# A list scheduler's landing times for GpSimd's transfers, and weight sums spread over fewer weights, in a hybrid transformer block

## The chip, the cores and the metric

The kernel runs on one core of a Trainium2 chip, in one launch. The metric is the device time of one execution in microseconds (us); several executions are timed and the median is compared. One further execution was taken with the hardware profiler. The engines are named as the profile names them: PE (matrix products; PEld is its weight load), DVE (vector), ACT (scalar and activations), POOL (GpSimd) and SP (which only issues transfers here).

## The reference

One layer on 256 tokens of width 2048, everything in float32: two SwiGLU blocks (5632 wide) around a gated recurrence, a second recurrence and a cross attention, each with a norm ahead of it and a residual sum behind it.

```python
x = x + 0.5 * swiglu(rms_norm(x, ffn1_norm[l]), ffn1_w_up[l], ffn1_w_down[l])
h = rms_norm(x, mix_norm[l])
proj = h @ w_in[l]
...
merged = g[:, :, 0, :] * (y_a @ w_branch_a[l]) + g[:, :, 1, :] * (y_b @ w_branch_b[l])
x = x + merged @ w_out[l]
x = x + cross_attention(rms_norm(x, xattn_norm[l]), rms_norm(mem, mem_norm[l]), xattn_wq[l], xattn_wkv[l], xattn_wo[l])
x = x + 0.5 * swiglu(rms_norm(x, ffn2_norm[l]), ffn2_w_up[l], ffn2_w_down[l])
return rms_norm(x, final_norm)
```

## The kernel before

**Tiles.** Every weight comes in pieces of 128 x 2048 float32 (1 MB), loaded by SP into a tile `raw`. ACT copies a piece to a rounded type (`h`), DVE subtracts that from the piece (`l`, what the rounding lost), and PE multiplies both parts with the two parts of the activations, so that three cheap products stand for one float32 product (`split`, L531). The pieces are used in one fixed order (`plan`): the first feed forward block (`ffn1`), 176 pieces of the middle (the input projection, gates, branches, output, and the attention's four weights), and the second block (`ffn2`). The function `weights` (L584) takes the next piece and prepares the one after.

**Fewer products by sums of weights.** In both feed forward blocks most pieces of the up projection take part in a scheme that needs seven products where eight were needed, but with four differences of blocks of the weight (tile `td`). In `ffn2`, 36 pieces (list `MADE`, L47) have these differences made ahead, in the middle of the kernel: POOL loads a piece from `wu2` into a tile `made`, DVE does four subtractions of 128 x 512 in it, and POOL stores it to a place in device memory, `kept` (`make_sums`, L611). Later SP loads it from there into `td`. `make_ahead` (L603) says at which weight each of the 36 is recorded: evenly over `between[1]` = 170 weights from the third of the middle on, the subtractions and the store two weights behind the load. In `ffn1`, 24 pieces have `l` made by another way: ACT writes the negative of the rounded piece and POOL issues a transfer that adds the piece to it (`begin_added`, L626).

**Tiles in rings.** All 1 MB tiles (`raw`, `h`, `l`, `td`, `tl`, `own`, `made`, `ev`) come out of one ring of 9 buffers, with 4 more inside the two feed forward blocks. A new tile takes a buffer whose last user is done, in the plan described next. On the chip, the first instruction that writes the tile waits on semaphores until that user is really done.

**The order.** Nothing is issued as it is written. Each call is recorded as an `Op` with a cost (`price`, L254): time on its engine (`busy`) and, for a transfer, the time for which it holds the memory path (`moved`, 2.9 us a MB, 5.2 with an addition). `arrange` (L290) then works out the order of all operations: it goes through planned time, and gives each free engine the ready operation that is due first, counting back from PE's use of it. For a transfer, planned time says that its data are there, or its source is free, at `dma + 1.9`, where `dma` is the planned end of its share of the memory path (L382); the same 1.9 us stands in `spent`, from which due times come (L296). The result is the order of instructions on each engine, and which buffer each tile gets. Planned times themselves are not in the program: engines run their instructions in that order, and wait for each other by semaphores alone. `emit` (L434) issues all of it from one line, L464, so that the profile shows every instruction with that line; tiles tell them apart.

Of the kernel before, what the change touches and what calls it, by code (L numbers as in the profile page):

```python
# [46 lines left out]
MADE = [(g, p) for g in range(1, NG) for p in range(8) if p not in ((4, 6) if g < 3 else (1, 2, 3, 5, 6))]  # L47
# [131 lines left out]
LAG = {"PE": 0.24, "DVE": 0.15, "ACT": 0.16, "POOL": 0.16, "SP": 0.1}  # L179
# [4 lines left out]
class Flow:  # L184
# [69 lines left out]
    def price(self, op, method, args, kw, outs):  # L254
        q = op.queue.name
        n = outs[0].cells.size if outs else 0
        if method == "dma_start":
            n = n or args[1].cells.size
            op.moved = n * 512 / 2 ** 20 * (5.2 if "accum_op" in kw else 2.9)
            op.busy = 0.9 if q == "POOL" else 0.06  # L260
        elif method == "transpose":
            op.busy += 0.099
        elif q == "PE":
            op.busy += n / 2400 + 0.0137 if not op.turn else 0.021 if n <= 32 else 0.07 + n * 1.05e-3
        elif q == "DVE":
            n = max(n, kw["in_"].cells.size) if method == "tensor_reduce" else n
            per = {"reciprocal": 6.2, "tensor_tensor_scan": 2.2}.get(method, 1.042)
            op.busy = n * per / 1000 + 0.07
        elif q == "ACT":
            op.busy = n * 0.838e-3 + 0.095 + (0.1 if "accum_out" in kw else 0)  # L270
            op.table = args[2] if args[2] in TABLES else None
        else:
            op.busy = 1.0
# [16 lines left out]
    def arrange(self):  # L290
# [2 lines left out]
        ops = self.ops  # L293
        for op in ops:
            op.after = [a for a in getattr(op, "extra", ())]
            op.spent = op.busy + LAG[op.queue.name] + (op.moved + 1.9 if op.moved else 0)  # L296
        for op in ops:
            op.waits = len(op.deps)
            for d in op.deps:
# [20 lines left out]
        dma = reached = 0.0  # L320
# [6 lines left out]
        def enter(op):  # L327
            if op.nominal > reached + AHEAD:
                heappush(later[op.queue.name], (op.nominal, op.i, op))
            else:  # L330
                insort(cand[op.queue.name], op, key=lambda o: (o.due, o.i))
# [8 lines left out]
        while events:  # L340
            t, e = heappop(events)
            if free[e] > t + 1e-9:
                continue
            while later[e] and later[e][0][0] <= reached + AHEAD:
                enter(heappop(later[e])[2])
            best, soon = None, 1e18
            for op in cand[e]:
                if best is not None and (not last or best.turn or op.due - STICK > best.due):
                    break
                if best is not None and not op.turn:  # L350
                    continue
                r = op.ready
                if op.moved:
                    r = max(r, dma - BACKLOG)
                if r <= t + 1e-9:
                    for ring in {x.ring for x in op.takes}:
                        fit = ring.fit(op, self)
                        r = max(r, fit[-1][0] if fit else 1e18)
                if r <= t + 1e-9:
                    best = op  # L360
                else:
                    soon = min(soon, r)
            if best is None:
                if soon < 1e17:
                    heappush(events, (soon, e))
                continue
            op = best
            cand[e].remove(op)
            op.start = t
            sequence.append(op)  # L370
            busy = op.busy
            if op.table is not None and op.table != table:
                table = op.table
                busy += 1.3
            if e == "PE":
                busy += 0.1 * (op.turn != last)
                last = op.turn
            free[e] = t + busy
            op.end = t + busy + LAG[e]
            if op.moved:  # L380
                dma = max(dma, t + busy) + op.moved
                op.end = dma + 1.9  # L382
            woken = {e}
            if e == "PE" and op.nominal > reached:
                reached = op.nominal
                woken.update(names)
            for ring in {x.ring for x in op.takes}:
                fit = ring.fit(op, self)
                for x in op.takes:
                    if x.ring is ring:  # L390
                        f = fit.pop(0)
                        ring.take(op, f)
                        x.place = f[1]
                        scope = ring.places[f[1]][0].scope
                        if scope is not None:
                            self.opened = max(self.opened, scope)
                            live[scope] += 1
                        if f[2] is not None:
                            for u in f[2].users:
                                if u is not op:  # L400
                                    u.extra.append(op)
                woken.update(names)
            if op.scope is not None:
                live[op.scope] -= 1
            for x in op.tiles:
                x.left -= 1
                x.ends = max(x.ends, op.end)
                if not x.left:
                    x.ring.free.append((x.ends, x.place, x))
                    if x.ring.places[x.place][0].scope is not None:  # L410
                        live[x.ring.places[x.place][0].scope] -= 1
                    woken.update(names)
            for s in op.after:
                kind = s.deps[op]
                if kind is None:
                    r = t
                elif s.queue is op.queue and not op.moved:
                    r = t + busy + (0.1 if kind and e in ("DVE", "ACT") else 0)
                else:
                    r = op.end  # L420
                s.ready = max(s.ready, r)
                s.waits -= 1
                if not s.waits:
                    enter(s)
                    woken.add(s.queue.name)
            for n in woken:
                heappush(events, (max(t, free[n]), n))
            done += 1
# [40 lines left out]
def block_kernel(tc: tile.TileContext, xT, xin, memT, vec, gfin, bgate, lruw, wu1, wd1, win, wv,  # L469
# [91 lines left out]
    between = len(plan)  # L561
# [16 lines left out]
    between = between + 2, len(plan) - between - 6  # L578
# [5 lines left out]
    def weights(*key):  # L584
        while plan and len(ahead) < 2:
            i = next(planned)
            k, src, kind = plan.pop(0)
            flow.room = room["scope"] if k[0] in orders else None
            if i < len(head):
                head[i]()  # L590
            if plan and plan[0][2] == "added":
                begun.append(begin_added(plan[0][1]))
            ahead.append((k, prepare(src, kind, 4 if i < 4 else 1)))
            if i in rest:
                rest[i]()
            make_ahead(i - between[0])
        k, w = ahead.pop(0)
        assert k == key, (k, key)
        return w
# [1 line left out]
    sums_kept, makers = {}, []  # L601

    def make_ahead(i):  # L603
        n, pieces = len(MADE), between[1]
        if 0 <= i < pieces:
            for j in range(i * n // pieces, (i + 1) * n // pieces):
                makers.append((i + 2, make_sums(*MADE[j])))
        while makers and (makers[0][0] == i or i == pieces):
            makers.pop(0)[1]()

    def make_sums(g, p):  # L611
        raw = big("made", F32)
        r = [raw[:, i * 512:(i + 1) * 512] for i in range(4)]
        gps.dma_start(raw, wu2[g, p])

        def sums():
            for o, a, b in ((1, 0, 1), (0, 0, 2), (2, 2, 1), (3, 3, 2)):
                dve.tensor_tensor(out=r[o], in0=r[a], in1=r[b], op=ALU.subtract)
            kept = sums_kept[g, p] = dram.tile([P, 2048], F32, name=f"kept{g}_{p}", tag=f"kept{g}_{p}")
            gps.dma_start(kept, raw)  # L620

        return sums
# [1033 lines left out]
```

## Time and profile before

| | |
|---|---|
| time, median of 3 executions | 2453.64 us (2452.77 to 2455.08) |
| profiled execution, its own time | 2456.57 us |
| profiled execution, span from first to last instruction | 2454.8 us |
| granted clock of PE, mean | 0.997 of full |
| memory read and written | 538.13 MB and 39.85 MB |

A row of a group view of the profile has the operation with the tile that it writes and those that it reads (`out<-in`), its size and count; behind the bar the busy time in us and the mean of one in ns; then for how long its engine stood idle just before such instructions, and what ended that. A row of the timeline has start and duration in us; in brackets stands the idle time of the engine before it, and whom it waited for. A row of waits has the sum of such idle times, their number and the longest. A row of the table by stretches has the stretch, its length, busy time and instructions of PE, PEld, DVE, ACT and POOL, then PE's granted clock, the busy share of the transfer engines, and GB/s. `acc` is a bank of PE's accumulators; SPq marks SP's queue of transfers.

### The profile page before, as it was taken

Reading aid. Unit: us, or ns where it says so; the run is one execution under the profiler, and the core shown is the slowest. Engines: PE = TensorE matmul, PEld = TensorE weight load, DVE = VectorE, ACT = ScalarE, POOL = GpSimd, SP = SyncE. Lnnn points to the kernel's source line nnn. Section 1 sums busy time; section 2 is a strip of 40 time slices with the busy share of each in tenths; the row PEclk is TensorE's granted clock in tenths of the full one; section 3 lists DMA queues with packets and bytes.
Section 4 is the critical chain, followed back from the end, with each engine's and each line's share of the span. In section 5 each row is a group of like instructions: output and inputs, shape, how many; then the busy total and the mean of one; then the engine's idle time right before and its main releaser. Section 6 shows DMA issues by size and latency. Waiting matters only on the chain. (4 is left out here: it accounts for less than half of the span.)

```text
span 2454.8 us, 30751 instructions
## 1 busy us (share of the span) xinstructions
PE 2423.6 (99%) x12166; PEld 2018.0 (82%) x12166; DVE 2010.7 (82%) x2171; ACT 1405.8 (57%) x1408; POOL 61.7 (3%) x102
## 2 busy tenths in 40 slices
PE   9999999999999999999999999999999999999998
PEld 8888888888888887888788788888878788888887
DVE  8999999999855767687676777667769999999995
ACT  8566666666654443576434644545646566666663
POOL 0000000000000000000000000000000000000000
PEclk9999999999999999999999999999999999999999
DMA  8567888778745566767777676666787666666672
GB/s 308 188 228 257 257 260 254 257 251 264 243 152 196 203 243 218 275 242 272 260 269 268 241 292 243 259 227 232 290 321 286 242 244 244 244 244 244 244 287 111
DMA packets 89712, 605.14 MB, mean 247 GB/s; under 512 B 9952, under 2 KB 10208, under 8 KB 21472
## 3 DMA queue, kind: packets, MB, share of 16 engines
q1 hardware_dynamic: 75024, 501.38, 55.5%
q0 software_dynamic: 13824, 100.67, 13.3%
q8 instruction: 95, 1.56, 0.2%
q10 hardware_dynamic: 720, 1.13, 0.1%
q14 instruction: 49, 0.40, 0.0%
HBM read 538.13 MB, written 39.85 MB: 235 GB/s over the span
## 5 line engine op out<-in xcount | busy, mean ns | idle before, releaser
L464 DVE TENSOR_TENSOR l<-raw,h 128x2048 fp32r<-128x2048 f32 (+2 forms) x428 | 875.7, 2051 | 226.3 <-ACT h L464 115.8
L464 ACT ACTIVATE h<-raw 128x2048 fp32r<-128x2048 f32 (+2 forms) x428 | 736.6, 1725 | 536.0 <-PE acc L464 145.1
L464 PE MATMUL acc<-h,xh 128*128 128x512 f32 x1248 | 469.9, 391 | 2.8 <-ACT h L464 2.4
L464 PE MATMUL acc<-h,xl 128*128 128x512 f32 x1248 | 449.9, 389 | 0.0
L464 PE MATMUL acc<-h,hidop 128*128 128x512 f32 x1408 | 442.2, 390 | 0.0
L464 PE MATMUL acc<-h,ops 128*128 128x512 f32 x1664 | 412.5, 392 | 1.2 <-DVE gate L464 1.2
L464 ACT ACTIVATE h<-td 128x1024 fp32r<-128x1024 f32 (+1 forms) x244 | 286.8, 1182 | 208.3 <-DVE td L464 182.8
L464 PE MATMUL acc<-ops,h 128*128 128x512 f32 x1152 | 392.7, 398 | 0.4 <-DVE ops L464 0.4
L464 PEld LDWEIGHTS acc<-h,ops 128*128 128x128 f32 x1664 | 311.1, 188 | 65.5 <-DVE gate L464 1.5
L464 DVE TENSOR_TENSOR tl<-td,h 128x1024 fp32r<-128x1024 f32 (+1 forms) x244 | 333.0, 1373 | 22.1 <-ACT h L464 14.4
L464 PEld LDWEIGHTS acc<-h,hidop 128*128 128x128 f32 x1408 | 262.9, 188 | 53.9 <-ACT ev L464 0.2
L464 PE MATMUL acc<-ops,l 128*128 128x256 f32 x1152 | 273.6, 282 | 8.1 <-DVE l L464 8.1
L464 PEld LDWEIGHTS acc<-h,xh 128*128 128x128 f32 x1248 | 233.5, 188 | 56.1 <-ACT h L464 7.4
L464 PEld LDWEIGHTS acc<-h,xl 128*128 128x128 f32 x1248 | 234.3, 188 | 48.6
L464 PE MATMUL acc<-l,hidop 128*128 128x512 f32 x704 | 265.8, 389 | 0.0
L464 PEld LDWEIGHTS acc<-ops,l 128*128 128x128 f32 x1152 | 213.4, 190 | 29.0 <-DVE l L464 9.0
L464 PEld LDWEIGHTS acc<-ops,h 128*128 128x128 f32 x1152 | 203.2, 189 | 32.1 <-DVE ops L464 0.7
L464 PE MATMUL acc<-l,ops 128*128 128x512 f32 x832 | 221.0, 389 | 0.0
L464 PE MATMUL acc<-l,xh 128*128 128x512 f32 x688 | 198.8, 390 | 0.0
L464 PEld LDWEIGHTS acc<-l,ops 128*128 128x128 f32 x832 | 155.6, 188 | 32.2
L464 PE MATMUL acc<-tl,xh 128*128 128x512 f32 x560 | 174.3, 391 | 0.3 <-DVE tl L464 0.2
L464 PEld LDWEIGHTS acc<-l,hidop 128*128 128x128 f32 x704 | 132.2, 188 | 27.4
(172 smaller groups left out, 1893.2 us busy)
## 6 DMA issues: line engine op xcount, KB each, us to landing
raw<-wu SPq DMA_DIRECT2D x128, 1024.0 KB, 6.8
raw<-wd SPq DMA_DIRECT2D x72, 1024.0 KB, 6.3
raw<-win SPq DMA_DIRECT2D x40, 1024.0 KB, 4.8
made<-wu POOLq DMA_DIRECT2D x36, 1024.0 KB, 5.2
kept<-made POOLq DMA_DIRECT2D x36, 1024.0 KB, 6.2
td<-kept SPq DMA_DIRECT2D x36, 1024.0 KB, 6.6
raw<-wg SPq DMA_DIRECT2D x32, 1024.0 KB, 5.4
raw<-wu SPq DMA_DIRECT2D x36, 768.0 KB, 4.3
```

The lines of the kernel that those rows point to most:

```text
L464: getattr(op.queue.real, method)(*map(real, args), **{k: real(v) for k, v in kw.items()})
```

## The change

Two constants of planned time and one count change; no operation is added or removed.

- Planned landing is now a number for each transfer, `lands`: 1.9 us as before where SP or ACT issues it, and for POOL's transfers 3.2 us where it adds (the 24 of `ffn1`), 4.6 us for a load into `made`, and 5.8 us for a store from `made` to `kept`. (The line tells the load by its tiles: it touches no tile but the one that it writes.) It stands in both places where 1.9 stood.
- `make_ahead` spreads the 36 loads of `made` over 154 weights where it had 170.

```diff
@@ -258,6 +258,7 @@
             n = n or args[1].cells.size
             op.moved = n * 512 / 2 ** 20 * (5.2 if "accum_op" in kw else 2.9)
             op.busy = 0.9 if q == "POOL" else 0.06
+            op.lands = 1.9 if q != "POOL" else 3.2 if "accum_op" in kw else 4.6 if op.tiles - {args[0].tile} == set() else 5.8
         elif method == "transpose":
@@ -293,7 +294,7 @@
-            op.spent = op.busy + LAG[op.queue.name] + (op.moved + 1.9 if op.moved else 0)
+            op.spent = op.busy + LAG[op.queue.name] + (op.moved + op.lands if op.moved else 0)
@@ -379,7 +380,7 @@
                 dma = max(dma, t + busy) + op.moved
-                op.end = dma + 1.9
+                op.end = dma + op.lands
@@ -601,7 +602,7 @@
     def make_ahead(i):
-        n, pieces = len(MADE), between[1]
+        n, pieces = len(MADE), between[1] - 16
         if 0 <= i < pieces:
             for j in range(i * n // pieces, (i + 1) * n // pieces):
                 makers.append((i + 2, make_sums(*MADE[j])))
```

Since the whole order is worked out from these numbers, nearly every row of it moves somewhat. Two places are shown, both on DVE, both with the numbers of the tiles.

The first is in the middle of the kernel, in the last part of the input projection. `made` are the subtractions for the fourth piece of `MADE`; `l` is the lower part of a weight that PE takes next; `ya`, `ostd` and `plain` belong to the recurrences. In the order before:

```order
L464 TENSOR_TENSOR made_7274<-made_7274 128x512
L464 TENSOR_TENSOR ya_7283<-acc_7220,ostd_7332 128x256
L464 RECIPROCAL ostd_7332<-ostd_7332 128x256
L464 SCALAR_TENSOR_TENSOR ya_7283<-ya_7283,vt_74,silu_5987 128x256
L464 TENSOR_TENSOR ya_7283<-acc_7221,ostd_7332 128x256
L464 TENSOR_TENSOR plain_7337<-plain_7337,rstd_5469 128x256
L464 SCALAR_TENSOR_TENSOR ya_7283<-ya_7283,vt_74,silu_5987 128x256
L464 TENSOR_TENSOR plain_7337<-acc_7285,lo_7399 128x256
L464 TENSOR_TENSOR plain_7337<-plain_7337,rstd_5469 128x256
L464 TENSOR_TENSOR l_7414<-raw_7217,h_7270 128x2048
```

In the order now, of the same piece:

```order
L465 TENSOR_TENSOR made_7230<-made_7230 128x512
L465 TENSOR_TENSOR l_7333<-raw_7243,h_7307 128x2048
L465 TENSOR_TENSOR plain_7350<-acc_7210,lo_7331 128x256
L465 RECIPROCAL ostd_7338<-ostd_7338 128x256
L465 TENSOR_TENSOR plain_7350<-plain_7350,rstd_5469 128x256
L465 TENSOR_TENSOR ya_7255<-acc_7219,ostd_7338 128x256
L465 RECIPROCAL ostd_7338<-ostd_7338 128x256
L465 TENSOR_TENSOR l_7384<-raw_7284,h_7343 128x2048
...
L465 SCALAR_TENSOR_TENSOR ya_7255<-ya_7255,vt_74,silu_5987 128x256
L465 TENSOR_TENSOR l_7424<-raw_7353,h_7406 128x2048
```

`l_7414` before and `l_7424` now lie in the buffer from which the `made` of this place was stored, at one and the same address; eight small operations stood between the last subtraction and the new tile, and now there are twelve (four of them left out above), two of them splits of whole weights into other buffers.

The second place is the last of the 36 pieces. In the order before, its four subtractions (`made_14290`) stand among the splits of `ffn2`, where `tl` is the lower part of a `td`:

```order
L464 TENSOR_TENSOR l_14284<-raw_14232,h_14266 128x1536
L464 TENSOR_TENSOR tl_14314<-td_14252,h_14301 128x2048
L464 TENSOR_TENSOR l_14333<-raw_14274,h_14320 128x2048
L464 TENSOR_TENSOR made_14290<-made_14290 128x512 x4
L464 TENSOR_TENSOR l_14365<-raw_14307,h_14352 128x1536
L464 TENSOR_TENSOR tl_14386<-td_14323,h_14373 128x2048
```

Now they (`made_13692`) stand in the attention's output product, where `xs` and `xl` are the first operands of `ffn2` in the making:

```order
L465 TENSOR_TENSOR xs_13744<-xg_13731,xs_13744 128x128
L465 TENSOR_TENSOR xl_13762<-xg_13731,xh_13755 128x512
L465 TENSOR_TENSOR made_13692<-made_13692 128x512 x3
L465 TENSOR_TENSOR xl_13753<-xs_13744,xh_13742 128x512
L465 TENSOR_TENSOR l_13786<-raw_13710,h_13772 128x2048
L465 TENSOR_TENSOR made_13692<-made_13692 128x512
```

`l_13786` is the first weight of `ffn2`; PE's first product of that block stands behind these rows in the program. No load of `made` and no subtraction is left inside `ffn2`.

## The prediction

> **What bounds the kernel now.** I read the share of the engines first, then what PE waits for, then the table by stretches.
>
> ```profile
> span 2454.8 us, 30751 instructions
> PE 2423.6 (99%) x12166; PEld 2018.0 (82%) x12166; DVE 2010.7 (82%) x2171; ACT 1405.8 (57%) x1408; POOL 61.7 (3%) x102
> PE acc L464 <- DVE l L464: 8.1, 2, 5.6
> PE acc L464 <- DVE merge L464: 3.4, 3, 1.6
> PE acc L464 <- ACT h L464: 2.4, 3, 1.3
> PE acc L464 <- DVE p L464: 2.0, 2, 1.4
> PE acc L464 <- DVE hidop L464: 1.5, 3, 0.7
> PE acc L464 <- DVE x L464: 1.2, 3, 0.6
> PE acc L464 <- DVE gate L464: 1.2, 1, 1.2
> PE warm L464 <- DVE ones L464: 1.1, 1, 1.1
> 829.00:1837.00 1008.00, 989.72 (x5452) 831.15 (x5451) 713.05 (x858) 510.26 (x596) 39.60 (x73) 0.99 0.70 259
> 2000.00:2050.00 50.00, 50.00 (x226) 41.22 (x225) 49.90 (x47) 31.35 (x26) 0.00 (x0) 1.00 0.65 234
> ```
>
> PE is the bound: it is busy for 99% of the span, and the change gives it the same products. So the change can only move PE's idle time. The eight rows of its waits add up to 8.1 + 3.4 + 2.4 + 2.0 + 1.5 + 1.2 + 1.2 + 1.1 = 20.9 us. The stretch from 829 to 1837 us, in which all 36 pieces are made ahead, holds 1008 - 989.7 = 18.3 us of it. There DVE is busy for 71% and the transfer engines for 70%: the waits are a matter of order and not of load. In `ffn2` (2000 to 2050 us) PE and DVE are both full and PE does not wait.
>
> **The change part by part: landings.** What the constants are about can be compared with the trace.
>
> ```profile
> made<-wu POOLq DMA_DIRECT2D x36, 1024.0 KB, 5.2
> kept<-made POOLq DMA_DIRECT2D x36, 1024.0 KB, 6.2
> l<-own POOLq DMA_DIRECT2D x24, 1024.0 KB, 8.2
> DVE made L464 <- DMA made<-wu: 32.6, 15, 4.3
> DVE l L464 <- DMA kept<-made: 18.8, 8, 5.6
> SPq L464 <- DMA kept<-made: 89.6, 17, 9.6
> ```
>
> The code before books a load of `made` and a store of `kept` alike, 0.9 to issue + 2.9 + 1.9 = 5.7 us, and an adding transfer 0.9 + 5.2 + 1.9 = 8.0. Now it books 0.9 + 2.9 + 4.6 = 8.4, 0.9 + 2.9 + 5.8 = 9.6 and 9.3. The medians of the last column (issue to landing) are 5.2, 6.2 and 8.2, so the old booking is short for about half of them, and the trace shows who pays: DVE stood 15 times before subtractions whose piece had not landed, and 8 times before a split whose buffer was still being stored. Mostly nobody needed DVE just then. Three times PE did.
>
> **A, 939 us.**
>
> ```profile
> 915.53 0.53 POOL L464 DMA_DIRECT2D made<-wu  x1 [19.14 <-PE acc L464]
> 923.03 1.42 DVE L464 TENSOR_TENSOR made<-made 128x512 f32<-128x512 f32 x2 [2.94 <-DMA made<-wu]
> 928.00 0.54 POOL L464 DMA_DIRECT2D kept<-made  x1 [11.93 <-DVE ya L464]
> 937.35 4.49 DVE L464 TENSOR_TENSOR l<-raw,h 128x2048 fp32r<-128x2048 f32 x2 [5.61 <-DMA kept<-made]
> 939.69 0.58 PE L464 MATMUL acc<-ops,l 128*128 128x256 f32 x1 [5.55 <-DVE l L464]
> 939.00:945.00 6.00, 5.31 (x18) 4.63 (x19) 6.00 (x4) 1.91 (x1) 0.00 (x0) 0.52 0.45 175
> ```
>
> The load took 923.0 - 915.5 = 7.5 us until DVE could begin, and the store 937.35 - 928.0 = 9.35; DVE lost 2.94 and 5.61 us to them, and PE, which needed that split, 5.55. Then PE's clock is down: 0.52 over six microseconds, of which PE ran 5.31, so 0.48 x 5.3 = 2.5 us more. The new bookings (8.4 and 9.6) cover both. The order now bears that out: behind the last subtraction stand, ahead of the split that takes this buffer, two splits into other buffers more than before. One such split costs 4.49 / 2 = 2.2 us, so DVE has 4.5 us more work to do while the store lands. That leaves 5.61 - 4.5 = 1.1 us, and DVE comes there with the 2.94 us of the load's wait saved. I take all: -5.55 - 2.5 = **-8.1**. If the wait only moved to the next split, it would be 0.
>
> On the clock the Trainium skill ("TensorE: Matmul & The Clock Gate", Part 1) says that PE falls to half clock after an idle window of about 3.4 us. For the 5.55 us here the trace agrees. For the two waits under D, of 1.6 us each, it would give no loss, and the trace shows one; by the page the sum would be 0.9 us smaller, and the measurement decides.
>
> **B, 1044 us, and C, 1403 us.**
>
> ```profile
> 1034.12 0.53 POOL L464 DMA_DIRECT2D made<-wu  x1 [10.72 <-PE acc L464]
> 1041.98 1.42 DVE L464 TENSOR_TENSOR made<-made 128x512 f32<-128x512 f32 x2 [2.70 <-DMA made<-wu]
> 1044.12 1.20 PE L464 MATMUL acc<-h,ops 128*128 128x512 f32 x4 [1.21 <-DVE gate L464]
> 1394.74 0.54 POOL L464 DMA_DIRECT2D kept<-made  x1 [11.80 <-DVE sum L464]
> 1401.33 2.29 DVE L464 TENSOR_TENSOR l<-raw,h 128x2048 fp32r<-128x2048 f32 x1 [1.55 <-DMA kept<-made]
> 1403.67 1.57 PE L464 MATMUL acc<-ops,l 128*128 128x256 f32 x11 [2.56 <-DVE l L464]
> ```
>
> B: subtractions 7.9 us behind the issue of their load (booked 5.7, now 8.4), and the gate product queued behind them on DVE. C: a split 6.6 us behind its store (booked 5.7, now 9.6). Both are covered: **-1.2** and **-2.6**.
>
> **D, 1211 us.**
>
> ```profile
> 1201.47 1.92 ACT L464 ACTIVATE h<-raw 128x2048 fp32r<-128x2048 f32 x1 [7.14 <-DMA raw<-wab]
> 1211.37 0.33 PE L464 MATMUL acc<-vt,merge 128*128 128x128 f32 x1 [1.56 <-DVE merge L464]
> 1213.30 0.98 PE L464 MATMUL acc<-vt,merge 128*128 128x128 f32 x7 [1.59 <-DVE merge L464]
> 1210.00:1218.00 8.00, 5.03 (x19) 3.99 (x20) 7.79 (x10) 1.09 (x2) 0.53 (x1) 0.79 0.79 297
> ```
>
> Weights came late (ACT stood 7.14 us for one), the splits ran into the merge, and PE lost 1.56 + 1.59 + 0.21 x 8 = 4.8 us. SP's queue waits for stores of `kept` 17 times in all, which a later booking avoids by giving loads other buffers; but PE waits for `merge` by its very chain. I take half, **-2.4**, with 0 and -4.8 as ends.
>
> **E, the spread: 1826 us.** One piece per 154/36 = 4.3 weights where it was 4.7, and the last ones no longer in `ffn2`.
>
> ```profile
> DMA packets 1940, 13.14 MB, mean 375 GB/s; under 512 B 209, under 2 KB 209, under 8 KB 721
> kept<-made POOLq DMA_DIRECT2D x1, 1024.0 KB, 11.8
> made<-wu POOLq DMA_DIRECT2D x1, 1024.0 KB, 9.3
> raw<-wu SPq DMA_DIRECT2D x2, 1024.0 KB, 11.6
> 1826.36 0.50 PE L464 MATMUL acc<-h,xh 128*128 128x512 f32 x1 [0.90 <-ACT h L464]
> 1830.97 0.50 PE L464 MATMUL acc<-h,xh 128*128 128x512 f32 x1 [1.33 <-ACT h L464]
> ```
>
> From 1800 to 1835 us (the first four rows are of that stretch) the transfers run at 375 GB/s, and single ones take 9 to 12 us. POOL's are 3 MB of the 13; without them, 3.1 MB / 375 GB/s = 8 us of transfers, the weights land earlier than PE waited: **-2.2**. The price is a denser middle. The 144 subtractions go by at 0.69 us at most (1.42 for two above), 99 us in 1008; at 170/154 the rate, that is 1.0 point of DVE's share more, beside 29% free, and the transfers rise from 259 to about 266 GB/s. I cost it at nothing; if that cover failed, what is pushed is a split of 2.2 us.
>
> **F, the rest of the order.** `ffn1`'s adding transfers are booked 1.3 us longer. They were booked right on the median, and PE waits there for little (at most the 1.5 us of `hidop`): 0. But a new order draws its small waits anew. Those not named above are 20.9 - 1.1 (start) - 5.55 - 1.2 - 2.6 - 3.15 - 2.2 = 5.1 us. At best none comes, at worst they take back all; I take some half of 5.1 as added, **+3**.
>
> Sum: -8.1 - 1.2 - 2.6 - 2.4 - 2.2 + 3 = -13.5 us on a span of 2454.8. The profiled execution itself took 2456.57, 2.9 above the median shown, so I take the difference and not the level: 2453.6 - 13.5 = **2440 us**. The floor is with no wait but the first: 20.9 - 1.1 + 2.5 + 1.7 = 24 us less, 2430.
>
> **The rivals.** *The old booking was long enough*, and what DVE waited for is contention, which goes wherever the transfers go. For it: E shows 9 to 12 us for transfers of one size. Against it: right behind A the transfer engines are busy for 0.45 only, and the stores' median is above 5.7. Then A to D reappear elsewhere, only E remains: about 2451 us.
>
> The Trainium skill ("DMA: Bandwidth & Descriptors", Anatomy of one DMA, SWDGE path) would have it so: by its fit, 2.0 us + bytes / 436e3, a transfer of 1 MB takes an estimated 4.4 us, which either booking covers. The medians here, 5.2 and 6.2, disagree.
>
> *Loads come late* (slower). A buffer of `made` is now booked 2.7 + 3.9 = 6.6 us longer in each of 36 rounds, out of nine buffers; SP then issues the weights' loads later, and where one lands late ACT, DVE and PE wait in turn, as at D, for 4.8 us each. It needs four such stalls to eat up A to E, and a fifth and sixth to be seen: some 2460 us. For it: the 7.14 us of ACT above, SP's 89.6 us. Against it: most of the booked time was spent waiting anyway, and the middle has 30% of its transfer time free.
>
> *All waits go* (faster): the order is right nearly everywhere, F is zero or below, D goes fully: 2432 us.
>
> **How the numbers follow.** A difference below about 0.2%, 4.9 us, can't be told from none here. The sum's case (2434 to 2447) gets 0.60, all waits gone 0.13, old booking enough 0.16, loads late 0.11. So faster 0.73; within 0.2%, 0.16; slower 0.11. The range for 8 of 10 goes from the floor's neighbour, 2431, to 2452, which takes in the second case.
>
> **What would show it.** In the waits, DVE's for `made` and for `kept` (32.6 and 18.8 us) fall below a third, and SP's 89.6 falls. PE's waits from 829 to 1837 us fall from 18 to some 5 us, and no stretch there has a clock of 0.5. From 1800 to 1835 us POOL issues nothing, and the raw weights land in under 9 us. Wrong would be: DVE's waits gone but PE's as long, for `h` behind late loads (the slower rival), or waits for `made` as before (the first). Wrong of another kind: a loss in `ffn2`, where DVE has nothing free and a start behind time would never be made up.

## The result, and the profile after

The changed kernel takes 2432.78 us (median of 4, 2430.61 to 2433.69) where the kernel before took 2453.72 beside it: 20.9 us or 0.85% less, ratio 0.9913 with a 95% interval of 0.9896 to 0.993. That lies inside the range, below the predicted 2440 and next to the case called "all waits go" (2432). The profiled execution took 2433.69 us, its span 2431.9, which is 22.9 less than the span before.

The page of the changed kernel, its first lines, then all of PE's waits (sum, number, longest):

```profile
span 2431.9 us, 30728 instructions
PE 2417.1 (99%) x12166; PEld 2014.7 (83%) x12166; DVE 2013.4 (83%) x2171; ACT 1410.1 (58%) x1408; POOL 61.5 (3%) x102
PE acc L465 <- DVE tl L465: 1.5, 2, 0.9
PE warm L465 <- DVE ones L465: 1.1, 1, 1.1
PE acc L465 <- DVE merge L465: 0.8, 1, 0.8
PE acc L465 <- ACT h L465: 0.5, 2, 0.3
PE acc L465 <- DVE hidop L465: 0.5, 1, 0.5
PE acc L465 <- ACT ev L465: 0.3, 1, 0.3
PE acc L465 <- DVE ops L465: 0.2, 1, 0.2
```

PE has the same 12166 products. Its waits fell from 21.5 us (the eight rows shown of before and two more, of 0.4 and 0.2 us) to 4.9. The waits on POOL's transfers, and the stretch in which the pieces are made, answer to the rows shown of before:

```profile
DVE l L465 <- DMA kept<-made: 0.9, 1, 0.9
DVE made L465 <- DMA made<-wu: 0.8, 1, 0.8
SPq L465 <- DMA kept<-made: 2.9, 2, 2.5
829.00:1837.00 1008.00, 1006.98 (x5560) 848.42 (x5559) 737.37 (x882) 526.46 (x606) 39.40 (x73) 1.00 0.73 266
```

DVE's 32.6 and 18.8 us have become 0.8 and 0.9, SP's 89.6 has become 2.9, and PE stands idle for 1.0 us of these 1008 where it was 18.3. The memory path runs at 266 GB/s there, up from 259, and PE pays nothing for it.

The place of term A, in the timeline of POOL and DVE:

```profile
912.28 0.53 POOL L465 DMA_DIRECT2D made<-wu  x1 [20.94 <-ACT osq L465]
923.96 0.54 POOL L465 DMA_DIRECT2D kept<-made  x1 [11.15 <-DVE made L465]
...
920.48 2.14 DVE L465 TENSOR_TENSOR made<-made 128x512 f32<-128x512 f32 x3
923.48 2.29 DVE L465 TENSOR_TENSOR l<-raw,h 128x2048 fp32r<-128x2048 f32 x1
929.95 2.23 DVE L465 TENSOR_TENSOR l<-raw,h 128x2048 fp32r<-128x2048 f32 x1
934.17 2.29 DVE L465 TENSOR_TENSOR l<-raw,h 128x2048 fp32r<-128x2048 f32 x1
```

The subtractions come 8.2 us behind the issue of their load and meet no wait (no bracket in their row). The split that takes the buffer of the store comes at 934.17, 10.2 us behind it, with the two other splits ahead of it, and meets none either. Work fills the time in which DVE stood before.

### The profile page after: what moved, and what is told of

Same layout as the page of the kernel before. It is cut to its first block, busy times and chain, and to the rows that moved or that the text cites. A ratio compares the mean times of both kernels' runs of the same rounds, so it can differ in the third digit from the quotient of the medians.

```text
span 2431.9 us, 30728 instructions
## 1 busy us (share of the span) xinstructions
PE 2417.1 (99%) x12166; PEld 2014.7 (83%) x12166; DVE 2013.4 (83%) x2171; ACT 1410.1 (58%) x1408; POOL 61.5 (3%) x102
## 4 chain that ended last, share of the span: by engine, by line
PE 90%; DVE 5%; DMA 2%; issue 2%; ACT 1%; ACTq 0%; DVEq 0%; SPq 0%
PE acc L465 90%; DVE l L465 2%; DVE td L465 1%; DVE tl L465 1%; DMA raw<-wab 1%; ACT h L465 1%; DMA raw<-wd 1%; DMA raw<-wu 1%; DVE ev L465 0%; DMA raw<-wg 0%; PE warm L465 0%; DVE x L465 0%; DVE hidop L465 0%; ACT x L465 0%; DVE made L465 0%
```

## The experiments

Each changes only the line of landings (`op.lands`) or the number of weights of the spread. Three theories were to be told apart: the bookings (short bookings make waits, and these reach PE), the spread, and the redraw (any other order would have done as well, since the order before met its waits by bad luck). For each kernel one row tells how long PE was busy from 780 to 1790 us, out of 1010; before and after have these, in this order:

```profile
780.00:1790.00 1010.00, 993.95 (x5711) 837.24 (x5710) 718.28 (x879) 507.54 (x602) 37.46 (x69) 0.99 0.69 252
...
780.00:1790.00 1010.00, 1008.98 (x5806) 851.97 (x5805) 733.75 (x896) 519.40 (x611) 39.40 (x73) 1.00 0.71 261
```

So PE stood idle there for 16.0 us before and 1.0 now.

### Landings alone, and the spread alone

```diff
-        n, pieces = len(MADE), between[1] - 16
+        n, pieces = len(MADE), between[1]
```

> The three new landings (3.2, 4.6, 5.8 us), the spread as before over 170 weights. Booking theory: the waits at A to D go, since they hang on the landings alone, and the waits at the start of ffn2 (2.2 us near 1826) stay: about 2436 us, 17 to 19 below before; DVE's waits for made and kept fall from 51 us to under 10. Spread theory: the gain came from the sums leaving ffn2 and the denser middle: about 2451 us. Redraw theory (the order before was an unlucky draw, and any other is better): about 2435 to 2445, with DVE's waits for made and kept still near 50 us.

Measured: 2436.45 us, ratio 0.9934 (0.9914 to 0.9953). In the profile, the middle and then the largest waits of PE at the start of `ffn2`:

```profile
780.00:1790.00 1010.00, 1009.80 (x5812) 852.88 (x5812) 731.86 (x892) 520.06 (x612) 37.93 (x70) 1.00 0.70 257
1806.67 0.73 PE L465 MATMUL acc<-h,xh 128*128 128x512 f32 x2 [0.95 <-ACT h L465]
1809.54 0.50 PE L465 MATMUL acc<-tl,xh 128*128 128x512 f32 x1 [0.75 <-DVE tl L465]
```

The middle is clean (0.2 us idle; DVE's waits for `made` and `kept` are 4.6 and 0.4 us) and the waits at 1806 and 1809 us stand, as the booking theory had it, also in its number.

```diff
-            op.lands = 1.9 if q != "POOL" else 3.2 if "accum_op" in kw else 4.6 if op.tiles - {args[0].tile} == set() else 5.8
+            op.lands = 1.9 if q != "POOL" else 1.9 if "accum_op" in kw else 1.9 if op.tiles - {args[0].tile} == set() else 1.9
```

> Spread over 154 weights, all landings 1.9 us as before. Booking theory: only the 2.2 us near 1826 go, DVE's waits for made and kept stay near 50 us, and PE keeps single waits of 2 to 6 us somewhere in the middle: 2445 to 2455 us. Spread theory: about 2433. Redraw theory: 2435 to 2445 though DVE's waits stay.

Measured: 2438.56 us, ratio 0.9945 (0.9927 to 0.9963).

```profile
PE acc L465 <- DVE l L465: 3.5, 2, 2.1
DVE made L465 <- DMA made<-wu: 22.5, 10, 4.0
DVE l L465 <- DMA kept<-made: 13.6, 5, 5.9
780.00:1790.00 1010.00, 1005.36 (x5785) 848.23 (x5784) 729.06 (x891) 516.35 (x609) 39.54 (x73) 1.00 0.70 259
```

The booking theory (2445 to 2455 us) missed this, and the redraw theory (2435 to 2445, with DVE's waits still there) had it. DVE still waits for 36 us, once for 5.9 us, a little longer than at A. But PE waits for `l` only twice, 2.1 us at most, and is idle for 4.6 us in the middle and not 16: the same kind of wait hits PE less in this order. So 13.9 us come off (2452.5 beside it) with the bookings as short as before. The next runs were made to see how far that goes.

### Loads alone, and stores alone

The landings were 5.8 us for stores and 1.9 for all else, and then 4.6 us for loads and 1.9 for all else, both with the spread of before:

```diff
+            op.lands = 1.9 if q != "POOL" else 1.9 if "accum_op" in kw else 1.9 if op.tiles - {args[0].tile} == set() else 5.8
...
+            op.lands = 1.9 if q != "POOL" else 1.9 if "accum_op" in kw else 4.6 if op.tiles - {args[0].tile} == set() else 1.9
```

> Landing 5.8 us for the stores to kept alone, 1.9 for loads into made and for the adding transfers, spread as before. Booking theory: DVE's waits for kept (18.8 us) and SP's (89.6 us) nearly vanish, its waits for made (32.6 us) stay; A loses the 5.55 us and the half clock, C and D most of theirs: about 2441 us. If the load's booking is what counts: above 2448.

> Landing 4.6 us for loads into made alone, 1.9 for stores and adding transfers, spread as before. Booking theory: DVE's waits for made nearly vanish, its waits for kept (18.8 us) and SP's (89.6 us) stay, and with them PE waits of several us: 2446 to 2451 us. If the load's booking is what counts: under 2441.

Measured: stores alone 2437.95 us, 0.9937 (0.9922 to 0.9951); loads alone 2434.75 us, 0.9928 (0.9913 to 0.9943). The waits and the middle of stores alone:

```profile
DVE made L465 <- DMA made<-wu: 38.3, 17, 6.5
SPq L465 <- DMA kept<-made: 36.3, 8, 7.6
780.00:1790.00 1010.00, 1009.34 (x5808) 851.98 (x5807) 727.51 (x887) 519.02 (x611) 37.94 (x70) 1.00 0.70 256
```

and of loads alone:

```profile
DVE l L465 <- DMA kept<-made: 8.3, 5, 3.1
DVE made L465 <- DMA made<-wu: 4.1, 2, 3.7
SPq L465 <- DMA kept<-made: 83.4, 23, 10.3
780.00:1790.00 1010.00, 1008.95 (x5806) 851.88 (x5806) 732.07 (x889) 521.63 (x612) 37.94 (x70) 1.00 0.70 257
```

Each booking does to its own waits what it should: with stores booked longer DVE meets no store at all, with loads booked longer its waits for loads go from 32.6 to 4.1 us. But each alone frees PE (0.7 and 1.1 us idle), while the other's waits stand: 38.3 us of DVE for loads in the one, 83.4 us of SP for stores in the other. So in these orders the waits that are left cost PE nothing, and the two terms don't add up. For loads alone the expectation (2446 at least) missed by 11 us. For stores alone the time came out 3 us below the expected 2441, and SP's waits fell to 36.3 us where they were to vanish nearly. Both edits also draw the order anew, so these runs don't tell whether it is the booking or the new order that spares PE.

### Other orders with short bookings

If any other order were as good, short bookings drawn anew would be too. All of POOL's landings were 1.8, 2.1 and 1.0 us, with the old spread:

```diff
+            op.lands = 1.9 if q != "POOL" else 1.8 if "accum_op" in kw else 1.8 if op.tiles - {args[0].tile} == set() else 1.8
...
+            op.lands = 1.9 if q != "POOL" else 2.1 if "accum_op" in kw else 2.1 if op.tiles - {args[0].tile} == set() else 2.1
...
+            op.lands = 1.9 if q != "POOL" else 1.0 if "accum_op" in kw else 1.0 if op.tiles - {args[0].tile} == set() else 1.0
```

> All of POOL's landings 1.8 us instead of 1.9, spread as before: a booking as short as before, but the order is drawn anew. Booking theory (short bookings are what costs): DVE's waits for made and kept stay near 50 us and PE's single waits in the middle stay, about 2448 to 2458 us. Redraw theory (the waits stay but the order before met PE with them by bad luck): DVE's waits stay near 50 us and the time is 2435 to 2445 us.

> All of POOL's landings 2.1 us, spread as before: a second redraw with a short booking. Booking theory: 2446 to 2456 us. Redraw theory: 2435 to 2445 us, with DVE's waits for made and kept near 45 us.

> All of POOL's landings 1.0 us, spread as before: the booking is 0.9 us shorter still. Booking theory: more waits than before for made and kept (60 to 90 us on DVE) and more of them reach PE: 2455 to 2475 us. Redraw theory: the number of waits rises alike, but what reaches PE is a matter of draw: 2436 to 2460 us, with no rule.

Measured: 1.8 us, 2451.82 (ratio 0.9994, 0.9981 to 1.0007: no change); 2.1 us, 2445.38 (0.997, 0.9956 to 0.9983); 1.0 us, 2477.54 (1.009, 1.006 to 1.0119: slower). The split of term A and PE's wait for it, in 1.8 and then in 2.1 us:

```profile
937.72 4.49 DVE L465 TENSOR_TENSOR l<-raw,h 128x2048 fp32r<-128x2048 f32 x2 [6.32 <-DMA kept<-made]
940.07 0.58 PE L465 MATMUL acc<-ops,l 128*128 128x256 f32 x1 [6.24 <-DVE l L465]
```

```profile
937.90 2.29 DVE L465 TENSOR_TENSOR l<-raw,h 128x2048 fp32r<-128x2048 f32 x1 [6.65 <-DMA kept<-made]
940.25 0.58 PE L465 MATMUL acc<-ops,l 128*128 128x256 f32 x1 [6.57 <-DVE l L465]
```

It is the same wait at the same place, but the order is hardly another one there: from 909 us up to this split, DVE's rows at 1.8 us are those of before, operation by operation, and at 2.1 us all but one pair of neighbours, which changed places. So these two runs show that this order meets its wait again, and say little about other orders. With 1.0 us the order differs more, and the split at 927 us that waits 5.81 us for a store holds up nothing on PE. The waits with 1.0 us for loads and stores and for the adding transfers of `ffn1`, then the table up to 780 us and for the middle:

```profile
DVE made L465 <- DMA made<-wu: 71.4, 28, 7.6
DVE l L465 <- DMA kept<-made: 25.9, 5, 9.9
PE acc L465 <- DMA l<-own: 12.6, 6, 2.5
PE acc L465 <- DVE merge L465: 11.8, 4, 6.1
0.00:780.00 780.00, 764.74 (x3455) 632.51 (x3456) 673.05 (x743) 503.05 (x484) 22.16 (x29) 0.99 0.71 236
780.00:1790.00 1010.00, 988.11 (x5669) 832.43 (x5668) 702.44 (x856) 493.61 (x587) 36.32 (x67) 0.99 0.66 244
```

The time falls as the booking grows: 2478, 2452 and 2445 us at 1.0, 1.8 and 2.1 us, with 2454 at 1.9 (before). But the 1.0 us were given to the adding transfers too: PE is idle for 15.3 us ahead of 780 us, where no `made` is loaded (2.2 before), and for 21.9 us in the middle (16.0 before). So much of its loss says nothing of loads and stores. And the spread alone, booked at 1.9 us too, took 2438.6: with bookings of 1.8 to 2.1 us an order takes anything from 2439 to 2454 us here, while with both loads and stores booked long five orders took 2432 to 2437 (the changed kernel, landings alone, and three below). Whether the order before was a bad draw is not settled by this.

### One store alone

The spread is that of before.

```diff
+            op.lands = 5.8 if isinstance(args[0], View) and args[0].tile.name == "kept1_3" else 1.9
```

> Landing 5.8 us for one store alone, that of the fourth piece (kept1_3, the wait of 5.6 us at 938); everything else books 1.9 us and 170 weights as before, and the order is the one before up to this place and again from about 1050 us on. Term A by itself: the wait of PE near 939 and the half clock behind it go, C, D and the waits near 1826 stay: 8 us less, 2444 to 2447 us. If PE only meets the wait at the next split, or the lost time is made up anyway by something else that is late: 2451 to 2455 us.

Measured: 2451.01 us, median of 12 (2444.17 to 2455.56), ratio 0.999 (0.9979 to 1.0001). The profiled execution, with 2447.08 us one of the faster ones, shows what was meant at A, and what came in its place at C:

```profile
932.35 2.29 DVE L465 TENSOR_TENSOR l<-raw,h 128x2048 fp32r<-128x2048 f32 x1 [0.89 <-PE acc L465]
...
1388.96 2.29 DVE L465 TENSOR_TENSOR l<-raw,h 128x2048 fp32r<-128x2048 f32 x1 [2.71 <-DMA kept<-made]
...
1391.31 2.72 PE L465 MATMUL acc<-ops,l 128*128 128x256 f32 x11 [3.76 <-DVE l L465]
780.00:1790.00 1010.00, 1001.84 (x5758) 844.49 (x5757) 721.99 (x881) 514.60 (x606) 38.05 (x70) 1.00 0.69 253
```

At A the split no longer waits for the store, and PE not for the split. PE's idle time in the middle halves (8.2 us), though C, with an order that had not changed, costs 1.2 us more than before, and the wait at the merge (D), likewise unchanged in order, is not there at all. Behind the longer wait at C the clock is down as well (0.79 from 1389 to 1397 us, where before it had no such loss). The span falls by 9.5 us: A gives its 8.1 and D, which cost 4.8 before, all of that, while C takes back 2.9. Without D's luck some 5 us would be left. Over twelve executions the edit is worth 2.5 us at the median, with an interval that just reaches 1, where 8 were expected: that is the other case of the expectation (2451 to 2455 us). Where the rest goes in the other executions is open: only one of them has a trace.

### The adding transfers, longer bookings still, and SP's

In order: 3.2 us for the adding transfers alone and all else as before; the changed kernel with 1.9 us for them; the changed kernel with 9.0 and 11.0 us for loads and stores; the changed kernel with 2.9 us for all of SP's and ACT's transfers.

```diff
+            op.lands = 1.9 if q != "POOL" else 3.2 if "accum_op" in kw else 1.9 if op.tiles - {args[0].tile} == set() else 1.9
...
+            op.lands = 1.9 if q != "POOL" else 1.9 if "accum_op" in kw else 4.6 if op.tiles - {args[0].tile} == set() else 5.8
...
+            op.lands = 1.9 if q != "POOL" else 3.2 if "accum_op" in kw else 9.0 if op.tiles - {args[0].tile} == set() else 11.0
...
+            op.lands = 2.9 if q != "POOL" else 3.2 if "accum_op" in kw else 4.6 if op.tiles - {args[0].tile} == set() else 5.8
```

> Landing 3.2 us for the adding transfers alone, all else as before. The middle of the order is as before, so A to E stay: 2452 to 2456 us, with 1 to 2 us more of PE waits ahead of 780 us than before. If the whole gain were a redraw of any kind: 2435 to 2445 us.

> The changed kernel with the adding transfers of ffn1 at 1.9 us again (loads 4.6, stores 5.8, spread over 154). After has 3.9 us of PE waits ahead of 780 us, before 2.2: if the 3.2 us made these, the waits there fall to about 2 us and the time is 1 to 2 us under that of the changed kernel: 2430 to 2433 us. If the adding landing matters for the gain: 2436 or more.

> Landings 9.0 us for loads into made and 11.0 us for stores (3.2 adding), spread over 154: above nearly every landing seen. Booking theory: nothing left to gain, no wait of DVE for made or kept at all, 2431 to 2436 us. If buffers held too long cost (the slower rival of the prediction): weights are issued later, PE waits for h and l in the middle, 2440 to 2460 us.

> The changed kernel with SP's landings at 2.9 us instead of 1.9 (booked 5.9 us a MB; the medians are 4.8 to 6.4). PE's waits from 829 to 1837 us are 1.0 us in the changed kernel, so little is left there: 2430 to 2434 us if ACT's waits for raw only shift; if weights booked longer crowd the ring of nine, PE waits again, 2436 to 2445 us.

Measured: 2452.35 (ratio 0.9998, 0.999 to 1.0006), 2432.24 (0.9914, 0.9901 to 0.9927), 2437.17 (0.9932, 0.9912 to 0.9952) and 2431.86 us (0.9914, 0.9899 to 0.9928). The adding transfers' booking brings nothing. The first 780 us, in the kernel before, the changed one and the one without their booking:

```profile
0.00:780.00 780.00, 777.77 (x3560) 646.55 (x3561) 682.29 (x749) 507.46 (x487) 22.13 (x29) 1.00 0.72 240
...
0.00:780.00 780.00, 776.10 (x3546) 643.50 (x3547) 682.21 (x746) 505.94 (x486) 22.12 (x29) 1.00 0.72 239
...
0.00:780.00 780.00, 777.68 (x3552) 645.53 (x3553) 681.85 (x748) 507.41 (x486) 22.15 (x29) 1.00 0.72 240
```

PE is idle there for 2.2, 3.9 and 2.3 us. It is a loss of 1.6 us in the profiles, below what the medians can tell. Of the very long bookings, the profile shows no wait of DVE for `made` or `kept` any more, and 3.9 us idle in the middle with one wait of 2.34 us for a residual sum at 1362 us; all four of its executions (2436.92 to 2437.69 us) lie above all four of the changed kernel, but the intervals of the two ratios overlap, so that a cost of buffers held too long is hinted at, not shown. No version is clearly better than the changed kernel.

## Why the prediction was right, point by point

- **What bounds the kernel** held: PE's work is unchanged, and the gain is idle time of PE given back. Of the 22.9 us between the spans, 21.5 - 4.9 = 16.6 are waits of PE, and 2.5 + 1.7 us the half clock behind A and D; 2.1 us are not put down to anything. The time lies inside the range, but 7 us below the sum's 2440, a third of the gain: the direction was right, the sum too careful.
- **A, B, C** went in the profile as the sum had them (-8.1, -1.2, -2.6): none of the three waits is there now, and no half clock in the middle (granted clock 1.00 in every 100 us from 800 to 1900). That the booking takes away the wait at A is shown by the run with one store, where the wait goes with that store's booking alone; but that edit brought 2.5 us at the median, so that A's price of 8.1 is not confirmed by itself.
- **Booking or order.** From 780 to 1790 us PE is idle for 4.6 to 21.9 us in the six kernels that book all loads and stores at 1.0 to 2.1 us, and for 0.2 to 1.2 us in six of the seven that book loads, stores or both longer throughout (4.0 with 9 and 11 us). That speaks for the bookings. But four of the six have A's order, or nearly (before, adding transfers alone, 1.8 and 2.1 us), and the spread alone took off 13.9 us without any longer booking. No run draws many orders at one booking, so how much of the gain another order would have brought by itself stays open.
- **The two bookings.** That the bookings of loads and stores each pay for their own term is not so: either one alone frees PE in the middle. Why the load's does it for stores too (the longest wait of DVE for `kept` fell from 5.6 to 3.1 us with the stores' booking as before) is open.
- **D** was taken by half, for the merge waits by its own chain. It went nearly whole: 0.8 us are left of 3.15, and the clock loss of 1.7 with it, so -4.0 and not -2.4. That the queue of SP was behind it is argued from its waits for stores, which fell from 89.6 to 2.9 us along with it. The run with loads alone speaks against that: SP waits 83.4 us for stores there, and PE not once for `merge`. The run with one store alone warns that D also comes and goes with the landing times of an execution. Its cause stays open.
- **E** was undersized. The two waits near 1826 us were the visible part; landings alone leave more waits there. From 1790 to 2420 us, landings alone and then the changed kernel:

```profile
1790.00:2420.00 630.00, 625.31 (x2783) 512.76 (x2782) 593.91 (x524) 378.93 (x300) 1.61 (x3) 1.00 0.67 249
...
1790.00:2420.00 630.00, 629.29 (x2806) 517.34 (x2806) 593.28 (x520) 380.18 (x302) 0.00 (x0) 1.00 0.66 243
```

  That is 4.7 against 0.7 us idle: the spread is worth 4 us there, and the medians differ by 3.7. In all, PE is idle there for 0.1 to 2.1 us in the five kernels with 154 weights and for 1.6 to 5.3 in the nine with 170. The mechanism was right: POOL issues nothing from 1800 to 1835 us now, and 10.24 MB move there where it was 13.14:

```profile
DMA packets 1553, 10.24 MB, mean 293 GB/s; under 512 B 176, under 2 KB 176, under 8 KB 688
```

  Of the raw weights there, one of 1 MB took 9.2 us, just above the 9 that the prediction named as a sign.
- **F** is the term that failed. It charged +3 us for waits that a new order would draw anew, in proportion to the small ones of before. But those of before were not all chance: they were 5.1 us (5.7 with the two rows that the prediction left out) and are 3.0 now (4.9 less the start's 1.1 and D's 0.8), the waits for `p` (2.0 us) and `x` are gone, and the whole middle has 1.0 us. A DVE that is not held up by transfers does not come late to the small chains either; this last step is argued from the waits going together, not tested, and with stores alone the wait for `p` is gone too, though DVE waits 38.3 us for loads. What was drawn anew is in `ffn1`, the part costed at nothing: 1.7 us.
- **The rivals.** "The old booking was long enough" is ruled out: booking POOL's transfers longer took away the waits for them, and the transfers are no shorter now taken together (a median of 5.4 us over loads and stores in both kernels; loads went from 5.2 to 6.1, stores from 6.2 to 5.0). The fit in the Trainium skill ("DMA: Bandwidth & Descriptors", Anatomy of one DMA, SWDGE path), an estimated 4.4 us, lies below all four medians of loads and stores. "Loads come late" did not happen at the new bookings; at 9 and 11 us it is at most a few us. "All waits go" is the case that came true, with 0.13 where the sum's case had 0.60: the sum was too careful in D and F, by 1.6 and 5.1 us (-2.1 where +3 stood).

## What to carry to other kernels

A list scheduler whose durations are right can still be undone by one constant, how long a transfer holds its data or its buffer: compare it with the issue-to-landing times in the trace, for each issuing engine by itself, and look for instructions that wait for transfers although the engine they stand on has time to spare. Book it above the median, since the waits that count come from the late ones; booked far above (9 and 11 us here) nothing was gained, and some 4 us may have been lost. A change to such a constant is not priced by adding up the waits that it removes: most never reached the bound engine, and two constants can each remove the same ones. Such a change also draws the whole order anew: to tell the constant from the draw, compare several really different orders at the same constant.

## What the runs showed of the hardware

- Landing times of POOL's 1 MB loads and stores went from 4.1 to 11.8 us in one execution of the kernel before. A kernel's executions may scatter less where its order has slack, which is suggested and not shown. In one session the kernel before took 2447.58 to 2457.54 us (23 executions) and the one with one store mended 2444.17 to 2455.56 (12), while the two with long bookings took 2429.48 to 2434.0 and 2430.47 to 2432.04 (5 each). But landings alone, booked long too, took 2433.55 to 2440.88 in four.
- Half clock does not need a long wait of PE. In the kernel with 1.0 us, behind a wait of 2.51 us, the clock was down for half of the next stretch:

```profile
301.95 0.50 PE L465 MATMUL acc<-l,xh 128*128 128x512 f32 x1 [2.51 <-DMA l<-own]
302.00:309.00 7.00, 7.00 (x24) 5.59 (x25) 7.00 (x7) 5.30 (x4) 0.88 (x1) 0.76 0.85 312
```

  The wait of 2.56 us at 1403 us in the kernel before had no such loss:

```profile
1400.00:1450.00 50.00, 47.44 (x272) 41.16 (x272) 34.85 (x43) 23.21 (x28) 2.13 (x4) 1.00 0.74 264
```

  So a wait of that size may cost 1.7 us more or nothing.
